# When the modulation vectors of a four-layer encoder are computed, on which engine, and into which PSUM banks an output projection is summed

## The chip, the core and the metric

One core of one Trainium2 chip runs the whole step; nothing is shared with other cores. The metric is the device time of one execution in microseconds (us), the median of several runs. The engines named below are TensorE (PE, with PEld for its weight loads), VectorE (DVE), ScalarE (ACT), GpSimd (POOL) and SyncE (SP, which issues the transfers).

## The reference, cut to what matters

The kernel computes one inference step of a four-layer encoder for two sequences at once: a prompt of 256 tokens and a sample of 64, so 320 token columns of width 1024. Each layer is three sub-layers: a gated feed-forward net (ffn1), a token mixer (retention in layers 0 and 3, pooling in layer 1, attention in layer 2) and a second feed-forward net (ffn2). Every sub-layer is modulated by three vectors that come from the conditioning vector of its sequence:

```
c_act = silu(c)
mod = c_act @ ada_w[i] + ada_b[i]                       # 9 vectors of 1024 a layer
sh1, sc1, g1, shm, scm, gm, sh2, sc2, g2 = split(mod, 9)
h = rmsnorm(x, norm_g[i, 0]) * (1.0 + sc1) + sh1
x = x + 0.5 * g1 * swiglu(h, ffn1_w_in[i], ffn1_w_out[i])
h = rmsnorm(x, norm_g[i, 1]) * (1.0 + scm) + shm        # then the mixer, gm; then sc2, sh2, g2
```

All is float32. With 36 vectors of 1024 x 1024 weights, the modulation reads 288 weight tiles of 512 KB, beside 690 of the main weights.

## The kernel before, in words

**The stream.** All main weights are laid out as 690 chunks, each of eight 128 x 128 tiles, in the order in which TensorE uses them; a chunk is one transfer of 512 KB (`Stream.load`, L265). Six raw buffers hold what has landed. A float32 product is made of three faster products of a high and a low part: ScalarE rounds a raw chunk to its high part `hi` (L277), VectorE subtracts to get the low part `lo` (L284), and TensorE does three matmuls per tile (`mm3`, L379 to L381). The splits run three chunks ahead of the use. `next_tiles` is the kernel's metronome: at the first tile of a chunk it splits `hi` three chunks ahead and runs what is due (`tick`), and in the middle of the chunk it does the same for `lo`.

**Sub-layers.** There are twelve, numbered 0 to 11 here. Each has an input stretch (projections from the normalised `x`, held as `xh` and `xl`, 320 token columns and two shift columns) and an output stretch (eight output blocks m = 0 to 7, each summed over all k tiles, then added to `x` in `residual`, L558 on VectorE). In a feed-forward net the input stretch has 44 chunks and the output stretch 22. In an input stretch VectorE reads each finished pair of PSUM banks (L593), multiplies (L614) and takes low parts (L415). The retention and the attention use `out_projection`: its first four blocks are summed in two cuts of k, so that the late k tiles can still be in the making, and the blocks 4 to 7 follow one at a time.

**PSUM.** The eight banks are two pairs `mm` (four banks, handed out pair by pair), three banks `wk`, and one bank `ada`. Tiles are tracked by pair: an instruction that writes one bank of a pair waits for the readers of the pair. `four_banks` puts blocks 0 and 1 in one pair and 2 and 3 in the other. `bank` takes a whole pair and uses its first half.

**Modulation.** A vector v = 3n (shift), 3n + 1 (gain) or 3n + 2 (gate) of sub-layer n is made in one of two ways, one weight tile at a time, eight tiles a vector. On TensorE (`ada_pe`, L460): four matmuls of 32 columns each into the `ada` bank, and at the end a transpose on VectorE (L465). On VectorE (`ada_dve`, L475): two multiply-and-sum instructions over 1024 columns, one for each sequence. The first two vectors are made on TensorE before the stream starts. `ada_plan` decides the rest: each vector has a due chunk, each chunk has some room for VectorE tiles (`ROOM_IN` in an input stretch, `ROOM_OUT` in an output stretch, `ROOM_RET` in a retention's input stretch), and a vector goes to VectorE if the room up to its due chunk holds its eight tiles; otherwise it goes to TensorE, spread evenly over the time left. The plan before puts four vectors, 4, 16, 19 and 28, on TensorE, and the other 30 on VectorE.

**Shift columns.** `shift_columns` (ACT L521, DVE L522) writes the next sub-layer's shift vector into two columns of `xh` and `xl`. It is called at the first tile of the output stretch.

Of the kernel before, what the change touches and what calls it, by code (L numbers as in the profile page):

```python
# [11 lines left out]
F32 = mybir.dt.float32  # L12
# [7 lines left out]
P = 128  # L20
D = 1024
KT = D // P
# [26 lines left out]


PE_STEP = 1
ROOM_IN = {"ffn": 0.42, "poo": 0.0, "att": 0.0}
ROOM_OUT = {"ffn": 0.6, "ret": 0.5, "poo": 0.0, "att": 0.3}
ROOM_RET = (1, 0, 0, 0, 0, 0, 0, 0, 0, 1, 2, 0)

# [13 lines left out]
def sub_tiles(kind, layer):  # L69

    j = layer // 3
    out = []
    if kind in ("ffn1", "ffn2"):
        wi, wo = kind + "_w_in", kind + "_w_out"
        for m in range(FT):
            for kt in range(KT):
                out.append((wi, layer, kt, m * P))
                out.append((wi, layer, kt, DFF + m * P))
        for m in range(KT):
            for kt in range(FT):  # L80
                out.append((wo, layer, kt, m * P))
    elif kind == "ret":
        for h in range(RH):
            for base, n, w in ((0, 2, RDK), (D, 2, RDK), (2 * D, 4, RDV), (4 * D, 4, RDV)):
                for m in range(n):
                    for kt in range(KT):
                        out.append(("ret_w_in", j, kt, base + h * w + m * P))
        out += [("ret_w_out", j, kt, m * P) for m, kt in out_order(4 * RH, RET_EARLY)]
    elif kind == "pool":
        for g in range(4):  # L90
            for kt in range(2):
                for m in range(2):
                    out.append(("pool_w", (j, g), kt, m * P))
    else:
        for hp, part in att_columns():
            for base in ((0, D), (2 * D,))[part]:
                for kt in range(KT):
                    out.append(("att_w_qkv", j, kt, base + hp * P))
        out += [("att_w_o", j, kt, m * P) for m, kt in out_order(NPAIR, ATT_EARLY)]
    return out  # L100


def out_order(nk, early):

    cuts = (0, *early, nk)
    out = [(m, kt) for a, b in zip(cuts, cuts[1:]) for m in range(4) for kt in range(a, b)]
    return out + [(m, kt) for m in range(4, KT) for kt in range(nk)]


def att_columns():  # L110

    out = [(0, 0), (1, 0), (0, 1), (1, 1)]
    for hp in range(2, NPAIR):
        out += [(hp, 0)] if hp >= ATT_LATE else [(hp, 0), (hp, 1)]
    return out + [(hp, 1) for hp in range(ATT_LATE, NPAIR)]


def chunk_starts(subs):
    starts, n = [], 0
    for kind, layer in subs:  # L120
        starts.append(n)
        n += len(sub_tiles(kind, layer)) // 8
    return starts, n


def ada_plan(subs):


    starts, total = chunk_starts(subs)
    due, room = {}, [0.0] * total  # L130
    for n, (kind, layer) in enumerate(subs):
        w_in = {"ffn1": 44, "ffn2": 44, "ret": 48, "att": 24, "pool": 0}[kind]
        due[3 * n + 2] = starts[n] + w_in
        if n + 1 < len(subs):
            due[3 * n + 3] = starts[n] + w_in
            due[3 * n + 4] = starts[n] + w_in
        size = len(sub_tiles(kind, layer)) // 8
        for c in range(size):
            if 3 <= c < size - 2:
                own = ROOM_IN if c < w_in else ROOM_OUT  # L140
                room[starts[n] + c] = ROOM_RET[c % 12] if kind == "ret" and c < w_in else own[kind[:3]]
    order = sorted(due)
    got = np.concatenate([[0.0], np.cumsum(room)])
    plan = {}
    on_pe, done = [], 0
    for v in order:
        if got[due[v] - 2] >= done + KT:
            for t in range(KT):
                done += 1
                c = max(1, int(np.searchsorted(got, done - 1e-6)) - 1)  # L150
                plan.setdefault(c, []).append(("d", v, t))
        else:
            on_pe.append(v)
    at = 1.0
    for i, v in enumerate(on_pe):
        rest = min((due[u] - 2 - at) / (KT / PE_STEP * (k + 1)) for k, u in enumerate(on_pe[i:]))
        for kt in range(0, KT, PE_STEP):
            plan.setdefault(int(at), []).append(("a", v, kt))
            at += max(0.0, rest)
    return plan  # L160


def ada_layout(subs):

    return {v: what for todo in ada_plan(subs).values() for what, v, _ in todo} | {0: "a", 1: "a"}
# [147 lines left out]
class Kernel:  # L313
# [74 lines left out]
        return self.banks()[:, 0]  # L388

    def four_banks(self):  # L390
        t = (self.banks(), self.banks())
        return [t[i // 2][:, i % 2] for i in range(4)]

    def twins(self, name, dt=F32, n=2):
        return self.twin.tile([P, n, TW], dt, tag="twin", name=name)
# [57 lines left out]
    def ada_pe(self, v, kts):  # L453
        nc = self.nc
        for kt in kts:
            if kt == 0:
                self.ada_ps = self.adap.tile([P, 256], F32, tag="ada", name="ada")
            t = self.stream.take(("a", v, kt))
            for j in range(4):
                nc.tensor.matmul(out=self.ada_ps[32 * j:32 * j + 32, :], lhsT=self.cpad[:, kt, :],  # L460
                                 rhs=t[:, 256 * j:256 * j + 256], start=kt == 0, stop=kt == KT - 1)
            self.stream.load()
        if kts[-1] == KT - 1:
            tr = self.small.tile([P, KT, 32], F32, tag="adat", name="adat", bufs=1)
            nc.vector.transpose(out=tr.rearrange("p t s -> p (t s)"), in_=self.ada_ps)  # L465
            o = self.mod.tile([P, KT, 2], F32, tag=f"mod{v % 3}", name="mod")
            self.ada_end(v, o, tr[:, :, 0:2])
# [135 lines left out]
    def ffn(self, n):  # L603
        nc = self.nc
        hid = []

        def evac(ps):
            g, u = self.normed(ps)
            self.shifted(g, AF.Silu)
            self.shifted(u)  # L610
            self.at(2, lambda: combine(g[:, 0:NT], u[:, 0:NT]))

        def combine(g, u):
            nc.vector.tensor_tensor(out=u, in0=u, in1=g, op=ALU.mult)  # L614
            self.parts_later(u, hid.append)

        self.begin()
        for m in range(FT):
            ps = self.banks()
            for kt in range(KT):  # L620
                for i in range(2):
                    hi, lo = self.stream.next_tile()
                    self.mm3(ps[:, i, 0:NB], hi, lo, self.xh[:, kt, 0:NB], self.xl[:, kt, 0:NB], kt == 0, kt == KT - 1)
            self.after_norm(1, lambda ps=ps: evac(ps))
        for m in range(KT):
            po = self.bank()
            for kt in range(FT):
                hi, lo = self.stream.next_tile()
                if m == 0 and kt == 0:
                    if n + 1 < len(self.subs):  # L630
                        self.shift_columns(n + 1)
                if kt >= len(hid):
                    self.flush()
                h, l = hid[kt]
                self.mm3(po[:, 0:NT], hi, lo, h, l, kt == 0, kt == FT - 1)
            self.residual(n, m, po)
# [174 lines left out]
    def out_projection(self, n, nk, early, operands):  # L811

        ps = dict(enumerate(self.four_banks()))
        for i, (m, kt) in enumerate(out_order(nk, early)):
            hi, lo = self.stream.next_tile()
            if i == 0 and n + 1 < len(self.subs):
                self.shift_columns(n + 1)
            if operands[kt] is None:
                self.flush()
            if kt == 0 and m >= 4:  # L820
                ps[m] = self.bank()
            h, l = operands[kt]
            self.mm3(ps[m][:, 0:NT], hi, lo, h, l, kt == 0, kt == nk - 1)
            if kt == nk - 1:
                self.residual(n, m, ps[m])
# [386 lines left out]
```

## Time and profile before

| what | us |
|---|---|
| median of 3 runs | 2734.98 (2732.3 to 2736.49) |
| the profiled execution's own time | 2739.32 |
| its span, first to last instruction | 2737.5 |
| PE busy | 2693.6 (98%) |
| DVE busy | 2132.6 (78%) |
| ACT busy | 1332.4 (49%) |

The times in the rows below come from the one profiled execution. Its span leaves 1.8 us of its own time outside, and its own time is 4.3 us above the median of the runs. Matmuls overlap: one lasts 0.31 us, and the next starts 0.15 us after it, so the distance between starts says what a matmul costs. In a timeline the release in brackets names the idle time before an instruction and what ended it.

### The profile page before, as it was taken

The numbers are of one execution on the slowest core, as the hardware profiler recorded it, in microseconds if no ns is written. First come the engines' busy times: TensorE is split into PE (matmuls) and PEld (weight loads), VectorE is DVE, ScalarE is ACT, GpSimd is POOL, SyncE is SP. The second block draws the span as 40 slices with busy tenths as digits, with TensorE's granted clock in tenths as the row PEclk, the third lists the DMA queues.
The fourth block names the chain that finished last, engine by engine and source line by source line (L and its number), as shares of the span: only waits on it lengthen the run. The fifth ranks groups of instructions, "written<-read, shape, count | busy, mean of one in ns | idle before, by whom it ended". The sixth has DMA issues, their size and how long they took to land.

```text
span 2737.5 us, 46828 instructions
## 1 busy us (share of the span) xinstructions
PE 2693.6 (98%) x18328; PEld 2595.7 (95%) x18328; DVE 2132.6 (78%) x3606; ACT 1332.4 (49%) x2393; POOL 69.9 (3%) x141
## 2 busy tenths in 40 slices
PE   7999999999999999999999999999999999999999
PEld 5999988899999998999999988999999998889999
DVE  5879777788888887889788777788888877756553
ACT  4554454445535544554554455555455444544552
POOL 0000000000000002000000021000000000000000
PEclk9999999999999999999999999999999999999999
DMA  8667555666676674666666644466766655544442
GB/s 330 228 226 244 167 187 171 207 206 218 217 230 209 215 232 161 226 218 234 207 215 224 208 156 129 155 218 209 237 197 213 226 185 170 174 150 146 150 153 94
DMA packets 150109, 543.64 MB, mean 199 GB/s; under 512 B 17872, under 2 KB 19152, under 8 KB 149632
## 3 DMA queue, kind: packets, MB, share of 16 engines
q1 hardware_dynamic: 142272, 517.51, 57.4%
q0 software_dynamic: 6464, 21.82, 2.4%
q8 instruction: 144, 2.36, 0.4%
q10 hardware_dynamic: 1152, 1.31, 0.1%
q14 instruction: 77, 0.63, 0.1%
HBM read 528.13 MB, written 12.44 MB: 197 GB/s over the span
## 4 chain that ended last, share of the span: by engine, by line
PE 58%; DVE 2%; ACT 1%; issue 1%; DVEq 0%; ACTq 0%
PE mm L379 18%; PE mm L380 18%; PE mm L381 18%; PE wk L723 1%; PE wk L754 1%; DVE lo L284 0%; DVE pr L1000 0%; ACT pr L994 0%; PE wk L1053 0%; PE wk L957 0%; PE wk L707 0%; DVE xt L558 0%; DVE xl L505 0%; PE ada L460 0%; PE wk L1035 0%
## 5 line engine op out<-in xcount | busy, mean ns | idle before, releaser
L379 PE MATMUL mm<-xh,hi 128*128 128x322 f32 x3776 | 1198.6, 317 | 3.1 <-DVE xt L558 1.2
L380 PE MATMUL mm<-xl,hi 128*128 128x322 f32 x3776 | 1171.7, 310 | 0.1
L381 PE MATMUL mm<-xh,lo 128*128 128x322 f32 x3776 | 1169.8, 310 | 0.0
L277 ACT ACTIVATE hi<-raw 128x1024 fp32r<-128x1024 f32 x690 | 726.8, 1057 | 732.6 <-PE mm L380 635.0
L284 DVE TENSOR_TENSOR lo<-raw,hi 128x1024 fp32r<-128x1024 f32 x690 | 840.9, 1222 | 249.9 <-ACT hi L277 238.9
L379 PEld LDWEIGHTS mm<-xh,hi 128*128 128x128 f32 x3776 | 713.0, 189 | 27.2 <-issue 21.9
L380 PEld LDWEIGHTS mm<-xl,hi 128*128 128x128 f32 x3776 | 714.4, 189 | 5.1 <-issue 4.8
L381 PEld LDWEIGHTS mm<-xh,lo 128*128 128x128 f32 x3776 | 714.5, 189 | 0.0
L475 DVE SCALAR_TENSOR_TENSOR junk<-raw,cb 128x1024 f32<-128x1024 f32 x480 | 586.4, 1222 | 8.6
L379 PE MATMUL mm<-part,hi 128*128 128x320 f32 x1728 | 537.6, 311 | 7.9 <-DVE xt L558 7.9
L381 PE MATMUL mm<-part,lo 128*128 128x320 f32 x1728 | 536.2, 310 | 0.0
L380 PE MATMUL mm<-part,hi 128*128 128x320 f32 x1728 | 533.7, 309 | 0.1
L599 ACT ACTIVATE twin<-twin 128x256 f32<-128x256 f32 (+1 forms) x944 | 328.8, 418 | 193.9 <-DVE twin L593 193.9
L379 PEld LDWEIGHTS mm<-part,hi 128*128 128x128 f32 x1728 | 325.8, 189 | 15.7 <-DVE xt L558 9.4
L380 PEld LDWEIGHTS mm<-part,hi 128*128 128x128 f32 x1728 | 326.0, 189 | 1.3 <-issue 1.0
L381 PEld LDWEIGHTS mm<-part,lo 128*128 128x128 f32 x1728 | 326.3, 189 | 0.0
L593 DVE TENSOR_TENSOR twin<-mm,rx 128x644 f32<-128x644 f32 (+1 forms) x240 | 195.4, 814 | 75.3 <-PE mm L381 74.6
L499 ACT ACTIVATE xh<-xt,mod 128x256 fp32r<-128x256 f32 x192 | 71.1, 421 | 204.5 <-DVE xt L558 202.9
L558 DVE SCALAR_TENSOR_TENSOR xt<-mm,mod,xt 128x256 f32<-128x256 f32 (+1 forms) x176 | 59.3, 378 | 61.5 <-PE mm L381 61.5
L412 ACT ACTIVATE part<-twin 128x320 fp32r<-128x320 f32 x176 | 81.2, 461 | 48.3 <-DVE twin L614 48.3
L614 DVE TENSOR_TENSOR twin<-twin 128x320 f32<-128x320 f32 x176 | 85.7, 490 | 23.2 <-ACT twin L599 18.8
L415 DVE TENSOR_TENSOR part<-twin,part 128x320 fp32r<-128x320 f32 x176 | 85.4, 485 | 1.1 <-ACT part L412 1.1
(162 smaller groups left out, 1130.2 us busy)
## 6 DMA issues: line engine op xcount, KB each, us to landing
raw<-in_wmain SPq DMA_DIRECT2D x690, 512.0 KB, 3.8
raw<-in_wada SPq DMA_DIRECT2D x288, 512.0 KB, 4.2
out_ret_p<-st POOLq DMA_DIRECT2D x16, 256.0 KB, 2.5
out_ret_s<-st POOLq DMA_DIRECT2D x16, 256.0 KB, 3.8
s<-in_s POOLq DMA_DIRECT2D x6, 512.0 KB, 6.3
fb<-in_fb POOLq DMA_DIRECT2D x8, 384.0 KB, 4.0
xt<-in_xt SPq DMA_DIRECT2D x1, 1280.0 KB, 10.3
out_v_o<-twin POOLq DMA_DIRECT2D x8, 160.0 KB, 4.0
```

Of the source, the lines that this page charges most:

```text
L277: self.nc.scalar.activation(out=hi, in_=t, func=AF.Copy)
L284: self.nc.vector.tensor_tensor(out=lo, in0=t, in1=hi.bitcast(F32), op=ALU.subtract)
L379: t.matmul(out=out, lhsT=hi, rhs=xh, start=start, stop=False)
L380: t.matmul(out=out, lhsT=hi, rhs=xl, start=False, stop=False)
L381: t.matmul(out=out, lhsT=lo, rhs=xh, start=False, stop=stop)
L412: self.nc.scalar.activation(out=hi, in_=src, func=AF.Copy)
L415: self.nc.vector.tensor_tensor(out=lo, in0=src, in1=hi.bitcast(F32), op=ALU.subtract)
L475: nc.vector.scalar_tensor_tensor(out=self.junk, in0=t, scalar=1.0, in1=self.cb[:, s], op0=ALU.mult, op1=ALU.mult, accum_out=self.modv[v][: ...
L499: self.nc.scalar.activation(out=self.xh[:, t, b:e], in_=self.x[:, t, b:e], func=AF.Copy, scale=g[:, t, s:s + 1])
L593: self.nc.vector.tensor_tensor(out=t[:, :, 0:NB], in0=ps[:, :, 0:NB], in1=self.rx[:, None, 0:NB].to_broadcast([P, n, NB]), op=ALU.mult)
L599: self.nc.scalar.activation(out=t[:, b:e], in_=t[:, b:e], func=func, bias=t[:, NT + s:NT + s + 1])
L614: nc.vector.tensor_tensor(out=u, in0=u, in1=g, op=ALU.mult)
```

## The change

It has three parts. The first concerns the plan: the room for VectorE tiles in a feed-forward input stretch goes from 0.42 to 0.54 per chunk; a shift vector is due three chunks before its sub-layer's predecessor ends instead of at the start of the output stretch (where that is later); and vectors are taken in the order of their due chunks rather than of their numbers. The plan that results puts all vectors but the first two on VectorE: 34 vectors, 272 tiles (before 240). A feed-forward input stretch then holds 22 VectorE tiles (before 17 or 18) and an output stretch 12 as before; the attention's output stretch holds 2 (before 1), in chunks 420 and 424 (before 422). The second: `shift_columns` is called at the first tile of block 7, the last output block, instead of at the first tile of the output stretch. The third: `four_banks` puts blocks 0 and 2 in one pair and 1 and 3 in the other, and block 4 of `out_projection` is summed in the `ada` bank (`spare_bank`), which is idle then.

```
-ROOM_IN = {"ffn": 0.42, "poo": 0.0, "att": 0.0}
+ROOM_IN = {"ffn": 0.54, "poo": 0.0, "att": 0.0}
...
+        size = len(sub_tiles(kind, layer)) // 8
         due[3 * n + 2] = starts[n] + w_in
         if n + 1 < len(subs):
-            due[3 * n + 3] = starts[n] + w_in
+            due[3 * n + 3] = starts[n] + max(w_in, size - 3)
             due[3 * n + 4] = starts[n] + w_in
...
-    order = sorted(due)
+    order = sorted(due, key=lambda v: (due[v], v))
...
     def four_banks(self):
+
         t = (self.banks(), self.banks())
-        return [t[i // 2][:, i % 2] for i in range(4)]
+        return [t[i % 2][:, i // 2] for i in range(4)]
+
+    def spare_bank(self):
+        return self.adap.tile([P, 512], F32, tag="ada", name="spare")
...
-                self.ada_ps = self.adap.tile([P, 256], F32, tag="ada", name="ada")
+                self.ada_ps = self.adap.tile([P, 512], F32, tag="ada", name="ada")[:, 0:256]
...
-                if m == 0 and kt == 0:
+                if m == KT - 1 and kt == 0:
                     if n + 1 < len(self.subs):
                         self.shift_columns(n + 1)
...
-            if i == 0 and n + 1 < len(self.subs):
+            if m == KT - 1 and kt == 0 and n + 1 < len(self.subs):
                 self.shift_columns(n + 1)
...
             if kt == 0 and m >= 4:
-                ps[m] = self.bank()
+                ps[m] = self.spare_bank() if m == 4 else self.bank()
```

Four lines were added above most of the code, so L593 of the kernel before is L597 of the changed one, L475 is L479, and so on; `mm3` keeps its lines.

On TensorE, at the end of the first chunk of sub-layer 0 (`mm_307` is a pair of banks, `hi_265` and `hi_289` the first two chunks, `ada_340` the bank of vector 4), there stood before:

```order
L379 MATMUL mm_307<-xh_111,hi_265 128x322
L380 MATMUL mm_307<-xl_112,hi_265 128x322
L381 MATMUL mm_307<-xh_111,lo_267 128x322
L460 MATMUL ada_340<-raw_275,cpad_115 32x256 [waits DMAHW2_49,PE_49]
L460 MATMUL ada_340<-raw_275,cpad_115 32x256 x3
L379 MATMUL mm_307<-xh_111,hi_289 128x322 [waits Activation_49]
L380 MATMUL mm_307<-xl_112,hi_289 128x322
```

and now:

```order
L379 MATMUL mm_307<-xh_111,hi_265 128x322
L380 MATMUL mm_307<-xl_112,hi_265 128x322
L381 MATMUL mm_307<-xh_111,lo_267 128x322
L379 MATMUL mm_307<-xh_111,hi_289 128x322 [waits Activation_49]
L380 MATMUL mm_307<-xl_112,hi_289 128x322
```

The four matmuls of a modulation tile are gone, here and at 31 other chunk starts; nothing takes their place on this engine.

On TensorE in the attention's output projection, where block 0 ends and block 1 goes on, and where block 2 ends and block 3 goes on (before, `mm_17734` is the pair of blocks 0 and 1, `mm_17735` that of 2 and 3):

```order
L381 MATMUL mm_17734<-part_17939,lo_17686 128x320
L379 MATMUL mm_17734<-part_17553,hi_17662 128x320 [waits DVE_49]
L380 MATMUL mm_17734<-part_17553,hi_17662 128x320
...
L381 MATMUL mm_17735<-part_17939,lo_17762 128x320
L379 MATMUL mm_17735<-part_17553,hi_17736 128x320 [waits DVE_49]
L380 MATMUL mm_17735<-part_17553,hi_17736 128x320
```

and now, from the end of block 0 (`mm_17640` is the pair of blocks 0 and 2, `mm_17641` that of 1 and 3):

```order
L381 MATMUL mm_17640<-part_17848,lo_17592 128x320
L379 MATMUL mm_17641<-part_17459,hi_17568 128x320
...
L381 MATMUL mm_17641<-part_17848,lo_17592 128x320
L379 MATMUL mm_17640<-part_17459,hi_17642 128x320 [waits DVE_49]
...
L381 MATMUL mm_17640<-part_17848,lo_17666 128x320
L379 MATMUL mm_17641<-part_17459,hi_17642 128x320 [waits DVE_49]
```

Blocks 1 and 3 went on only behind the readers of the block that had just ended. Now block 1 goes on at once, block 2 waits for the readers of block 0, and block 3 for those of block 1: one block later in each case.

On VectorE at the end of the attention (`pr_17333` before and `pr_17239` now are the scores of the last pair of heads, `part` the parts of a finished pair, `lo` a chunk's low part), before:

```order
L997 TENSOR_SCALAR pr_17333<-pr_17333,sm_17782 128x256
L405 TENSOR_TENSOR part_17809<-wk_17796,part_17809 128x320 [waits DMASW3_49,Activation_49]
L284 TENSOR_TENSOR lo_17848<-raw_17360,hi_17824 128x1024 [waits DMAHW7_49,PE_49,Activation_49]
L1000 SCALAR_TENSOR_TENSOR pr_17333<-wk_17857,rq_17596,fs_17326 64x384 [waits DMASW2_49,DMASW3_49,PE_49,Pool_49]
L1000 SCALAR_TENSOR_TENSOR pr_17333<-wk_17857,rq_17596,fs_17326 64x384
```

and now:

```order
L1001 TENSOR_SCALAR pr_17239<-pr_17239,sm_17686 128x256
L409 TENSOR_TENSOR part_17713<-wk_17700,part_17713 128x320 [waits DMASW3_49,Activation_49]
L479 SCALAR_TENSOR_TENSOR junk_110,mod_17716<-raw_17266,cb_301 128x1024 [waits DMAHW1_49]
L479 SCALAR_TENSOR_TENSOR junk_110,mod_17716<-raw_17266,cb_301 128x1024 [waits DVE_49]
L284 TENSOR_TENSOR lo_17757<-raw_17347,hi_17733 128x1024 [waits DMAHW2_49,PE_49,Activation_49]
L1004 SCALAR_TENSOR_TENSOR pr_17239<-wk_17766,rq_17502,fs_17232 64x384 [waits DMASW2_49,DMASW3_49,PE_49,Pool_49]
L1004 SCALAR_TENSOR_TENSOR pr_17239<-wk_17766,rq_17502,fs_17232 64x384
```

A modulation tile, two instructions, now stands between the finished part and the scores of the sample for the last pair of heads. Before, the only such tile of this output stretch stood behind the residual of block 0.

## Rows read from the trace of the kernel before

**Rows 1.** The page, part 1: busy us, share of the span, instructions of each engine.

```profile
PE 2693.6 (98%) x18328; PEld 2595.7 (95%) x18328; DVE 2132.6 (78%) x3606; ACT 1332.4 (49%) x2393; POOL 69.9 (3%) x141
```

**Rows 2.** The page, part 4: shares of the chain that ended last, by engine.

```profile
PE 58%; DVE 2%; ACT 1%; issue 1%; DVEq 0%; ACTq 0%
```

**Rows 3.** Timeline of PE around one modulation tile: start us, us, what, idle before.

```profile
908.54 0.30 PE L381 MATMUL mm<-xh,lo 128*128 128x322 f32 x1
908.78 0.64 PE L460 MATMUL ada<-raw,cpad 128*32 128x256 f32 x8
909.35 0.41 PE L379 MATMUL mm<-xh,hi 128*128 128x322 f32 x1
909.60 0.31 PE L380 MATMUL mm<-xl,hi 128*128 128x322 f32 x1
```

**Rows 4.** Windows of PE: stretch, its length, busy us (matmuls), granted clock, DMA.

```profile
62.73:73.49 10.76, 10.76 (x74) 1.00 0.73 249
854.89:905.10 50.21, 50.21 (x338) 1.00 0.65 211
912.99:962.45 49.46, 49.46 (x338) 1.00 0.63 211
1820.74:1899.65 78.91, 78.91 (x531) 1.00 0.66 213
```

**Rows 5.** Waits of PE in the output projections of sub-layers 1, 10 and 7.

```profile
PE mm L379 <- DVE xt L558: 2.6, 2, 1.8
PE mm L379 <- DVE xt L558: 1.5, 2, 0.8
PE mm L379 <- DVE xt L558: 3.8, 2, 3.0
```

**Rows 6.** Timeline of PE and DVE in the output projection of sub-layer 1.

```profile
536.47 0.31 PE L381 MATMUL mm<-part,lo 128*128 128x320 f32 x1
537.83 0.67 DVE L558 SCALAR_TENSOR_TENSOR xt<-mm,mod,xt 128x256 f32<-128x256 f32 x2
538.56 0.41 PE L379 MATMUL mm<-part,hi 128*128 128x320 f32 x1 [1.78 <-DVE xt L558]
```

**Rows 7.** Windows of PE in the half-clock stretches behind two waits.

```profile
539.40:542.80 3.40, 3.40 (x15) 0.50 0.77 277
1720.40:1727.20 6.80, 5.70 (x21) 0.50 0.41 141
```

**Rows 8.** Windows of DVE: input and output stretch of sub-layer 9, input stretch of 11.

```profile
1992.40:2133.80 141.40, 120.71 (x170) 1.00 0.65 207
2133.80:2211.00 77.20, 68.69 (x114) 1.00 0.72 235
2515.10:2656.50 141.40, 84.36 (x102) 1.00 0.44 148
```

**Rows 9.** Lines of DVE in the input stretch of sub-layer 9: busy us, mean ns.

```profile
L284 DVE TENSOR_TENSOR lo<-raw,hi 128x1024 fp32r<-128x1024 f32 x40 | 48.9, 1222 | 11.1 <-ACT hi L277 9.8
L475 DVE SCALAR_TENSOR_TENSOR junk<-raw,cb 128x1024 f32<-128x1024 f32 x33 | 40.3, 1222 | 0.6
L593 DVE TENSOR_TENSOR twin<-mm,rx 128x644 f32<-128x644 f32 x20 | 16.5, 827 | 6.4 <-PE mm L381 6.3
L614 DVE TENSOR_TENSOR twin<-twin 128x320 f32<-128x320 f32 x21 | 10.2, 489 | 2.6 <-ACT twin L599 2.3
L415 DVE TENSOR_TENSOR part<-twin,part 128x320 fp32r<-128x320 f32 x21 | 10.2, 485 | 0.2 <-ACT part L412 0.2
```

**Rows 10.** Timeline of DVE around one modulation tile.

```profile
58.12 1.22 DVE L475 SCALAR_TENSOR_TENSOR junk<-raw,cb 128x1024 f32<-128x1024 f32 x1
60.54 0.82 DVE L593 TENSOR_TENSOR twin<-mm,rx 128x644 f32<-128x644 f32 x1
```

**Rows 11.** Timeline of DVE and PE at the end of the attention.

```profile
1708.31 0.42 DVE L997 TENSOR_SCALAR pr<-pr,sm 128x384 f32<-128x384 f32 x1
1709.97 0.87 PE L1035 MATMUL wk<-cst,pr 128*128 128x128 f32 x6
```

More of the change, by code (lines that the diff above doesn't have):

```diff
@@ L132, in ada_plan @@
         w_in = {"ffn1": 44, "ffn2": 44, "ret": 48, "att": 24, "pool": 0}[kind]
+        size = len(sub_tiles(kind, layer)) // 8
         due[3 * n + 2] = starts[n] + w_in
         if n + 1 < len(subs):
-            due[3 * n + 3] = starts[n] + w_in
+            due[3 * n + 3] = starts[n] + max(w_in, size - 3)
             due[3 * n + 4] = starts[n] + w_in
-        size = len(sub_tiles(kind, layer)) // 8
         for c in range(size):
```

## The prediction, written before the changed kernel ran

> **What bounds the kernel now.** I read the busy shares first: TensorE 98%, VectorE 78%, ScalarE 49% [rows 1]. Then the chain that ended last: TensorE holds 58% of it and no other engine over 2% [rows 2]. So time goes where TensorE's own work goes, plus the few places where it waits. Three things on TensorE are not the main product. (a) Modulation tiles, which I looked for in its timeline [rows 3]. (b) A slower beat of the main matmuls in some stretches, seen by comparing windows that hold equal numbers of matmuls [rows 4]. (c) Waits in the three out projections with two cuts, from the list of waits [rows 5], and behind two of them a granted clock of one half [rows 7]. After that I looked at the engine that gets more work, VectorE: how full its stretches are [rows 8], and of what [rows 9].
>
> **The change part by part.**
>
> *Modulation tiles leave TensorE.* A matmul of the main product starts 0.15 us after the one before. Across a modulation tile the distance is 908.54 to 909.35, 0.81 us, and the next one is 0.25 (909.35 to 909.60) [rows 3]: 0.66 + 0.10 = 0.76 us lost per tile. The plan takes away four vectors of eight tiles: 32 x 0.76 = 24.3 us. All stand inside the stream, where TensorE is busy throughout, so the whole of it counts. Their transfers stay: the same 512 KB tiles go through the same raw buffers and are only read by VectorE.
>
> *The slower beat.* In sub-layer 3, 338 matmuls last 50.21 us behind the first modulation tile of the stretch and 49.46 us behind the second: 1.5% [rows 4]. The same alternation goes through every feed-forward input stretch that holds modulation tiles: slow after an odd one, normal after an even one. There are ten such slow stretches, the first at 62.73 us and the last, of 78.91 us, ending at 1899.65 [rows 4]; they make up 344 us. Without modulation tiles I expect none: 344 x 0.015 = 5.1 us. I know no cause, only the coincidence, so the lower bound is 0.
>
> *The pairing of the blocks.* TensorE waits 2.6, 1.5 and 3.8 us in the three output projections, six waits, all for the residual of the block that has just ended [rows 5]. The case at 538.56 shows how: block 2's last matmul starts at 536.47, its residual only at 537.83, and block 3 stands until 538.56, though it writes another bank of the pair [rows 6]. From start to start that is 2.09 instead of 0.15 us, 1.94 lost where 1.78 is listed; and the matmul behind a wait costs about 0.10 more, as in rows 3. So the six cost 7.9 + 6 x 0.26 = 9.5 us. Behind the wait of 1.78 us the clock is granted at 0.50 (1.2 of 2.4 GHz) for 3.4 us, in which 15 matmuls run; behind the one of 3.0 us for 6.8 us, with 21 matmuls in 5.70 busy us [rows 7]. At the full beat these would take 2.2 and 3.1 us: 1.2 + 2.6 = 3.8 us more. The waits of 0.77 left the clock alone. Now a block waits for the residual of the block before the last, one block (3 us in the retention, 1.8 in the attention) later. The residual at 537.83 was 1.2 us late, so I take all six waits as gone, and the clock's falls with them: 9.5 + 3.8 = 13.3 us. Bounds: half of it, 6.6, if block 3 still finds block 1's residual late, and 13.3.
>
> *The spare bank.* Block 4 never waits in the trace of before: no matmul at its start is among the six. Taken alone it is worth 0; with the new pairing it keeps block 4 from waiting for block 2's residual. Bounds 0 and 1.1 us, a wait of 0.77 as in rows 5 with its 0.3 of restart.
>
> *VectorE gets 32 tiles more, where?* A tile costs 2.42 us of its queue (58.12 to 60.54) [rows 10]. In an input stretch it is busy 84.36 of 141.40 us without tiles, and 120.71 with 33 multiply instructions, 16.5 tiles [rows 8, 9]: 2.2 us each. With 22 tiles it will be 84.4 + 48.4 = 132.8 of 141.4, 94%. The output stretches keep their 12 tiles at 68.69 of 77.20, 89% [rows 8], and show no wait of TensorE for them. `lo` is made three chunks (10.5 us) ahead and a bank pair has 7 us until its next use, so a backlog of one tile hides. I charge 0. If the cover were gone, each wait costs as above, 1.1 to 5.8 us.
>
> The Trainium skill would charge more here: VectorE: DVE Perf Modes, section "The DRAIN you can't avoid", says that the next operation does not start until the pipeline has emptied, so that whole durations add up. By that the rows of the input stretch, 48.9 + 16.5 + 10.2 + 10.2 = 85.8 us [rows 9], and 22 tiles of 2 x 1.222 give 139.6 of 141.4 us, before any wait. The trace differs: those four rows and the 40.3 of the multiplies sum to 126.1 us, while the engine was busy in 120.71 [rows 8], so neighbours overlap.
>
> *One of the added tiles meets a chain.* In the attention's output stretch the tile of chunk 420 now stands ahead of the last pair's sample scores: 2.4 us on a chain that ended on VectorE at 1708.73, while TensorE came for it (the second of the two turns that start at 1709.97) at about 1710.4 [rows 11]. Slack 1.7, so 0.7 us is lost; less the gap of 0.4 that VectorE had in front of the scores, 0.3 to 0.4. I take 0.4; bounds 0 and 2.4. The tile that leaves chunk 422 stood ahead of block 1's residual, for which block 3 now waits.
>
> *Shift columns.* The same two small instructions, later; they are needed 22, 16 or 8 tiles on. The shortest lead, 8 tiles of three matmuls of 0.15 us, is 3.5 us, and in front can stand one `lo` (1.222) and one tile (2.42): 3.6 us. So 0, with 0.1 us as the other end. Pooling takes the new pairing too: its first output bank waits for one more ScalarE copy, 0 to 1.1 us; I take 0.
>
> *Sum.* 24.3 + 5.1 + 13.3 - 0.4 = 42.3 us. On the profiled execution's own 2739.3 us that makes 2697.0. The runs have a median of 2735.0, 4.3 below it, so for the runs I forecast 2735.0 - 42.3 = 2692.7, say **2693 us**.
>
> **The rivals.**
>
> *Part of the bank waits or the slow beat stays.* For it: VectorE was late by a whole residual at 537.83 [rows 6], and I do not know what makes the beat. Against it: with one block of distance that lateness is covered, and a stretch with no modulation tile on TensorE keeps the beat. Half the waits back is -6.6, the beat kept -5.1: 2698 to 2705 us.
>
> *VectorE becomes the bound of the input stretches.* By whole durations (the rule above) it would be at 139.6 of 141.4, and what it waits for others no longer fits: 6.4 + 2.6 us of idle time in front of two of its rows [rows 9] would push each of seven input stretches over by up to 7 us. For it: 94% leaves little. Against it: the overlap, and output stretches that run at 89% without a wait. Between 10 and 45 us back: 2703 to 2738 us.
>
> *Slower: the evacuations come late and the clock falls.* One mechanism: a pair of banks in an input stretch is read too late, TensorE stands as at 538.56 and then runs at half clock as in rows 7. One such event costs 2.0 + 1.2 = 3.2 us. It decides when VectorE's backlog passes the 7 us between uses of a pair, three tiles in a row. To turn the gain of 42 round takes 14 events, two in each of the seven input stretches; three in each are 21 x 3.2 = 67 us, 2760 us. Against it: the plan places at most two tiles in neighbouring chunks there, and before shows no wait of TensorE in an input stretch of a feed-forward net.
>
> **How the numbers follow.** The forecast (2684 to 2698) has 0.70; the first rival 0.19; VectorE as the bound 0.08; slower 0.03. The range goes to the far ends of the first rival, 2705, and some way into the second, 2712, and below to 2684, where the waits cost more than I counted or VectorE's later work runs earlier: 2684 to 2712. A measurement of this kernel can tell 0.2%, 5.5 us, from no change. Faster by more: the forecast, the first rival and most of the second, 0.95. Same, out of the second: 0.02. Slower: 0.03.
>
> **What would show it.** Right: no L464 matmul after the first 35 us; windows of 338 matmuls of 49.5 us everywhere in input stretches; no wait of `mm` for `xt` in the output projections; clock 1.00 at the ends of sub-layers 1 and 7; VectorE busy about 133 of 141 us in an input stretch. Wrong: waits of TensorE for L597 (the evacuation) or `lo` inside input stretches, or a wait at block 3.

## The result, and the profile after

The changed kernel takes 2700.97 us (median; 2700.73 to 2702.38), the kernel before, beside it on the same chip, 2735.73 us (2732.3 to 2739.15). The ratio is 0.9875, 95% interval 0.9863 to 0.9887: faster. The profiled execution of the changed kernel took 2702.38 us with a span of 2700.6; the span of before was 2737.5, so 36.9 us have gone between the two traces. The forecast was 2693 us; the time lies in the range, 8 us above the forecast.

The page's busy times after (part 1, as [rows 1]):

```profile
PE 2661.8 (99%) x18072; PEld 2584.2 (96%) x18072; DVE 2193.4 (81%) x3730; ACT 1326.4 (49%) x2393; POOL 69.6 (3%) x141
```

TensorE has 256 records fewer, 32 tiles of four matmuls with two records each, and is busy 31.8 us less. VectorE has 60.8 us more, which is less than 32 tiles of 2.42 us make (77.4): its instructions overlap.

The beat is even now. Two windows of PE in the input stretch of sub-layer 3 (columns as in [rows 4]):

```profile
839.80:889.20 49.40, 49.40 (x338) 1.00 0.74 233
889.20:938.60 49.40, 49.40 (x337) 1.00 0.71 226
```

Before, the first part of this stretch took 50.21 us for the same number [rows 4]. The out projection of sub-layer 1, in the timeline of DVE and PE (as [rows 6]):

```profile
526.11 0.67 DVE L562 SCALAR_TENSOR_TENSOR xt<-mm,mod,xt 128x256 f32<-128x256 f32 x2
...
527.73 0.31 PE L379 MATMUL spare<-part,hi 128*128 128x320 f32 x1
```

Block 2's residual comes at 526.11, while block 3 runs on, and block 4 starts in the spare bank without a wait. In the list of PE's waits from 475 to 560 us one row is left, and in sub-layer 10 none:

```profile
PE mm L379 <- ACT xh L525: 0.3, 1, 0.3
```

That one is new: sub-layer 2 waits for its shift columns. VectorE in the input and the output stretch of sub-layer 9 (windows, columns as in [rows 8]), and its lines in the input stretch:

```profile
1957.50:2098.90 141.40, 131.85 (x194) 1.00 0.70 227
2098.90:2176.10 77.20, 67.50 (x110) 1.00 0.73 238
```

```profile
L479 DVE SCALAR_TENSOR_TENSOR junk<-raw,cb 128x1024 f32<-128x1024 f32 x44 | 53.8, 1222 | 0.8
L284 DVE TENSOR_TENSOR lo<-raw,hi 128x1024 fp32r<-128x1024 f32 x40 | 48.8, 1219 | 4.5 <-ACT hi L277 4.1
L597 DVE TENSOR_TENSOR twin<-mm,rx 128x644 f32<-128x644 f32 x20 | 16.5, 824 | 1.1 <-PE mm L381 1.1
L618 DVE TENSOR_TENSOR twin<-twin 128x320 f32<-128x320 f32 x21 | 10.2, 488 | 2.6 <-ACT twin L603 2.6
L419 DVE TENSOR_TENSOR part<-twin,part 128x320 fp32r<-128x320 f32 x21 | 10.2, 485 | 0.2 <-ACT part L416 0.2
```

VectorE is busy in 131.85 of 141.40 us with 22 tiles, and TensorE waits for it nowhere in these stretches. What is left in front of its rows is smaller than before [rows 9]: 4.5 us at `lo` where 11.1 were, 1.1 at L597 where 6.4 were. The five rows alone sum to 139.5 us; they fit into 131.85 only because neighbours overlap.

New waits stand at the end of the attention. Here are the first three of the five rows in the list of PE's waits from 1670 to 1725 us (us in total, times, longest); the first two of them stand in the place of the third group of [rows 5]:

```profile
PE mm L379 <- DVE xt L562: 2.1, 1, 2.1
PE mm L379 <- ACT xh L525: 1.9, 1, 1.9
PE wk L1039 <- ACT vt L973: 1.3, 1, 1.3
```

Rows chosen from the timeline of DVE, ACT and PE there (start us, us, what; in brackets the idle time before it):

```profile
1695.92 0.08 DVE L479 DVE_READ_ACCUMULATOR junk<-raw,cb 128x1 f32 x1
1695.92 0.67 DVE L562 SCALAR_TENSOR_TENSOR xt<-spare,mod,xt 128x256 f32<-128x256 f32 x2
1696.43 0.75 ACT L503 ACTIVATE xh<-xt,mod 128x256 fp32r<-128x256 f32 x2 [4.10 <-DVE xt L562]
1697.44 1.04 ACT L277 ACTIVATE hi<-raw 128x1024 fp32r<-128x1024 f32 x1
1698.52 1.23 DVE L284 TENSOR_TENSOR lo<-raw,hi 128x1024 fp32r<-128x1024 f32 x1 [0.46 <-ACT hi L277]
1699.67 0.67 DVE L562 SCALAR_TENSOR_TENSOR xt<-mm,mod,xt 128x256 f32<-128x256 f32 x2
1700.48 0.39 PE L379 MATMUL mm<-part,hi 128*128 128x320 f32 x1 [2.07 <-DVE xt L562]
...
1703.41 0.67 DVE L562 SCALAR_TENSOR_TENSOR xt<-mm,mod,xt 128x256 f32<-128x256 f32 x2
1703.92 0.75 ACT L503 ACTIVATE xh<-xt,mod 128x256 fp32r<-128x256 f32 x2 [1.69 <-DVE xt L562]
1704.93 1.04 ACT L277 ACTIVATE hi<-raw 128x1024 fp32r<-128x1024 f32 x1
1705.88 0.20 ACT L525 ACTIVATE xh<-mod 128x16 fp32r<-128x16 f32 x1
1706.13 0.41 PE L379 MATMUL mm<-xh,hi 128*128 128x322 f32 x1 [1.90 <-ACT xh L525]
```

Here the reader sees a loop over two engines. A residual on VectorE (1695.92) lets ScalarE make the next operand and, behind it in its queue, the split `hi` (1697.44); `hi` lets VectorE make `lo` (1698.52), and only behind `lo` comes the next residual (1699.67). One turn is 3.75 us, while TensorE needs 3.51 us for a block. A modulation tile ends at 1695.92, ahead of block 4's residual; nothing behind it can catch up. Block 7 waits 2.07 us for the bank of block 5. The shift columns (L525), which used to be made at the first tile of the projection, now stand behind the last `hi`, and sub-layer 8's first matmul waits 1.90 us for them. Behind that the clock is granted at one half, 1.2 of 2.4 GHz (window of PE, columns as in [rows 7]):

```profile
1707.10:1710.50 3.40, 3.40 (x15) 0.50 0.49 154
```

Where the 36.9 us came from, from start to start of the chunks' first matmuls in both traces:

| place | gained, us | forecast |
|---|---|---|
| modulation tiles and even beat, all sub-layers | 29.6 | 29.4 |
| output projections of sub-layers 1 and 10 | 6.7 | 6.3 |
| attention, waits of blocks 1 and 3 with clock | 6.9 | 6.9 |
| attention, before its output projection | 1.6 | 0 |
| attention, tile of chunk 420 | -1.4 | -0.4 |
| attention, block 7's wait | -2.2 | 0 |
| sub-layer 8's start: wait, then half clock | -2.2, -1.7 | 0 |
| sub-layer 2's start | -0.6 | 0 |

They add up to 36.7. The -1.4 is from the experiment without that tile, below. The fourth row is a stretch in which the traces of the other kernels lie 0.4 to 2.7 us below before; its cause stays open.

### The profile page after: what moved, and what is told of

The parts are those of the page before. It is cut to its first block, busy times and chain, and to the rows that moved or that the text cites. A ratio compares the mean times of both kernels' runs of the same rounds, so it can differ in the third digit from the quotient of the medians.

```text
span 2700.6 us, 46421 instructions
## 1 busy us (share of the span) xinstructions
PE 2661.8 (99%) x18072; PEld 2584.2 (96%) x18072; DVE 2193.4 (81%) x3730; ACT 1326.4 (49%) x2393; POOL 69.6 (3%) x141
## 5 line engine op out<-in xcount | busy, mean ns | idle before, releaser
L479 DVE SCALAR_TENSOR_TENSOR junk<-raw,cb 128x1024 f32<-128x1024 f32 x544 | 664.3, 1221 | 9.5
L379 PE MATMUL mm<-part,hi 128*128 128x320 f32 x1688 | 521.9, 309 | 2.1 <-DVE xt L562 2.1
L381 PE MATMUL mm<-part,lo 128*128 128x320 f32 x1688 | 522.8, 310 | 0.0
L380 PE MATMUL mm<-part,hi 128*128 128x320 f32 x1688 | 519.4, 308 | 0.1
L379 PEld LDWEIGHTS mm<-part,hi 128*128 128x128 f32 x1688 | 316.6, 188 | 5.2 <-issue 4.5
L380 PEld LDWEIGHTS mm<-part,hi 128*128 128x128 f32 x1688 | 316.9, 188 | 1.3 <-issue 1.0
L381 PEld LDWEIGHTS mm<-part,lo 128*128 128x128 f32 x1688 | 317.0, 188 | 0.0
L597 DVE TENSOR_TENSOR twin<-mm,rx 128x644 f32<-128x644 f32 (+1 forms) x240 | 194.8, 812 | 35.6 <-PE mm L381 35.2
L618 DVE TENSOR_TENSOR twin<-twin 128x320 f32<-128x320 f32 x176 | 85.8, 489 | 24.3 <-ACT twin L603 22.0
```

What stands on the lines that cost most here:

```text
L379: t.matmul(out=out, lhsT=hi, rhs=xh, start=start, stop=False)
L380: t.matmul(out=out, lhsT=hi, rhs=xl, start=False, stop=False)
L381: t.matmul(out=out, lhsT=lo, rhs=xh, start=False, stop=stop)
L479: nc.vector.scalar_tensor_tensor(out=self.junk, in0=t, scalar=1.0, in1=self.cb[:, s], op0=ALU.mult, op1=ALU.mult, accum_out=self.modv[v][: ...
L597: self.nc.vector.tensor_tensor(out=t[:, :, 0:NB], in0=ps[:, :, 0:NB], in1=self.rx[:, None, 0:NB].to_broadcast([P, n, NB]), op=ALU.mult)
```

## The experiments

Each ran beside the kernel before, whose median was 2736.19 us (2733.76 to 2738.29) beside the first four and 2733.41 (2732.26 to 2736.22) beside the next three.

**The pairing of blocks undone.** The changed kernel with

```
-        return [t[i % 2][:, i // 2] for i in range(4)]
+        return [t[i // 2][:, i % 2] for i in range(4)]
...
-                ps[m] = self.spare_bank() if m == 4 else self.bank()
+                ps[m] = self.bank()
```

> The changed kernel with the old pairing of blocks (0 with 1, 2 with 3) and no spare bank. Theory (the loop residual - operand parts on ScalarE - low part paces the end of the attention, so the pairing gains nothing lasting there): the retentions lose what the pairing gave, 4.65 us in sub-layer 1 and 2.06 in sub-layer 10; the attention's output stretch gets its two waits of before back but loses most of the new ones at block 7 and at the shift columns, 0 to 2 us on balance: 2708 to 2710 us for the run, 6.7 to 8.7 above the changed kernel. Rival (each wait stands for itself, and the new ones come from the tile in chunk 424 alone): attention worse by 5.8 us more, 2713 to 2714 us.

Measured: 2709.4 us (2708.72 to 2709.9), ratio 0.9904 (0.9889 to 0.9919): 8.4 above the changed kernel, though the pairing had brought 6.7 + 6.9 us to their places. PE's waits from 1675 to 1730 us:

```profile
PE mm L379 <- ACT xh L525: 1.9, 1, 1.9
PE mm L379 <- DVE xt L562: 1.9, 2, 1.1
```

Sub-layers 1 and 10 lose 4.2 and 2.1 us again, the attention only 1.5 (0.9 of it before its output projection): with the old pairing the waits of blocks 1 and 3 come back, block 7's goes, and the one for the shift columns stays. So in the attention of the changed kernel, which has a modulation tile at chunk 424 and late shift columns, what the pairing gains at one block is given back a few blocks later. That this need not be so shows below, where the tiles are gone.

**The pairing alone.** The kernel before with the first of the two lines above in its new form (no spare bank, no other change).

> The kernel before with the new pairing of blocks alone (plan, shift columns and banks otherwise as before; block 4 takes a pair of its own). Theory of the paced loop: sub-layers 1 and 10 lose 4.65 and 2.06 us, the attention 1 to 3 us: 8 to 10 us below before, about 2726. Rival (the pairing is worth its full 13.3 us): 2722. In both the modulation tiles on TensorE and the slow beat stay.

Measured: 2730.01 us (2725.49 to 2730.85), ratio 0.9976 (0.9967 to 0.9986), so 6.2 us, where 8 to 10 were expected. Sub-layer 10 gains its 2.05, the attention 5.2 (2.1 of it before its output projection, 3.1 in it). Of the two waits in the attention one is left, in the list of PE's waits from 1650 to 1760 us:

```profile
PE mm L379 <- DVE xt L558: 2.0, 1, 2.0
```

It stands in front of block 3, which waits for block 1's residual, and that stands behind the modulation tile of chunk 422; the clock falls behind it too. This costs 3.8 us against the kernels without a tile in that place, and so the pairing brings its full 6.9 us in the attention only together with the new plan, which moves this tile. Sub-layer 1 gains only 1.06: what blocks 1 and 3 gain is taken back by a modulation tile on TensorE. The timeline there (SPq and POOL: the issue of a transfer):

```profile
538.87 0.33 SPq L265 DMA_DIRECT2D raw<-in_wada  x1
539.04 0.54 POOL L841 DMA_DIRECT2D win<-in_win  x1 [3.79 <-PE mm L381]
...
547.83 0.64 PE L460 MATMUL ada<-raw,cpad 128*32 128x256 f32 x8 [1.98 <-DMA raw<-in_wada]
```

This tile's transfer was issued beside the 896 KB that pooling loads, and came 8.9 us later, where the median is 4.2. In the kernel before it came as late (issued 539.66, landed 548.16), but TensorE arrived at 550.40, held up by the very waits that the pairing removes. That the two transfers slow each other is not tested. The wait costs the half clock again (granted 0.51 in the 3.40 us from 548.90). In the changed kernel no modulation tile is left on TensorE there, and the gain stays: the parts need each other.

**No tiles in the attention's output, and its shift columns early.** The changed kernel with

```
-ROOM_OUT = {"ffn": 0.6, "ret": 0.5, "poo": 0.0, "att": 0.3}
+ROOM_OUT = {"ffn": 0.6, "ret": 0.5, "poo": 0.0, "att": 0.0}
...
-            if m == KT - 1 and kt == 0 and n + 1 < len(self.subs):
+            if (i == 0 if nk == NPAIR else m == KT - 1 and kt == 0) and n + 1 < len(self.subs):
```

> The changed kernel with two edits in the attention's output stretch: no modulation tile there (room 0), and the shift columns written at its first tile again. Theory (the tile of chunk 424 delays the residual of block 4 and so of block 5, for which block 7 waits; the shift columns stand in ScalarE's queue behind a late residual; the clock falls behind these two waits): the 2.2, 2.1 and 1.7 us of chunks 426 to 428 go, 6.0 us, 2695 us for the run. Rival (the loop is late by itself, with no tile in it): block 7 still waits, 2697 to 2699 us.

Measured: 2694.12 us (2692.84 to 2697.32), ratio 0.985 (0.9836 to 0.9865); it beats both kernels. Its timeline of VectorE, residuals of the attention's blocks 3 to 7:

```profile
1686.22 0.67 DVE L562 SCALAR_TENSOR_TENSOR xt<-mm,mod,xt 128x256 f32<-128x256 f32 x2
1689.97 0.67 DVE L562 SCALAR_TENSOR_TENSOR xt<-spare,mod,xt 128x256 f32<-128x256 f32 x2
1693.72 0.67 DVE L562 SCALAR_TENSOR_TENSOR xt<-mm,mod,xt 128x256 f32<-128x256 f32 x2
1697.47 0.67 DVE L562 SCALAR_TENSOR_TENSOR xt<-mm,mod,xt 128x256 f32<-128x256 f32 x2
1701.22 0.67 DVE L562 SCALAR_TENSOR_TENSOR xt<-mm,mod,xt 128x256 f32<-128x256 f32 x2
```

The loop's 3.75 us are still there. Without a tile in it the residuals fall only 0.24 us further behind with each block, and no block waits for one; sub-layer 7 takes 181.06 us instead of 187.79 (1.15 of the difference lies before its output projection), sub-layer 8 234.17 instead of 235.85, and the clock does not fall between them.

**Only the shift columns early.** The second of these edits alone.

> The changed kernel with the shift columns of the sub-layer after the attention written at the first tile of its output stretch again; the modulation tiles stay. Theory: the 1.9 us in front of the first matmul of sub-layer 8 goes, the 2.1 us at block 7 stay; whether the clock still falls behind block 7's wait is open: 2697.4 us if it does not, 2699 if it does. Rival (another late thing takes the place of the shift columns, such as the high part of block 0 of the next operand): no change, 2701.

Measured: 2698.89 us (2698.05 to 2702.96), ratio 0.9871 (0.9855 to 0.9887). In its list of PE's waits from 1660 to 1720 us

```profile
PE mm L379 <- DVE xt L562: 2.1, 1, 2.1
```

stays, and the one for `xh` is gone with the half clock, as in the first of the two cases forecast: sub-layer 8 takes 234.17 us, and the output stretch of sub-layer 7 44.26 instead of 46.03.

**Only the tiles gone.** The first of these edits alone.

> The changed kernel without modulation tiles on VectorE in the attention's output stretch (they move to the stretches behind); the shift columns stay at the last output block. Theory (two mechanisms, added up): the tile of chunk 420 cost 1.4 us ahead of the last sample scores and the tile of chunk 424 made block 7 wait 2.1 us for block 5; both go, while the first matmul of sub-layer 8 still waits about 1.9 us for the shift columns, which ScalarE makes late, with the half clock behind it: sub-layer 7 at about 183.5 us, sub-layer 8 at 235.8, 2697 us. Rival (the tiles alone made ScalarE late, so that the late shift columns do no harm by themselves): the wait for the shift columns and the half clock go too: sub-layer 7 at 181 to 182 us, sub-layer 8 at 234.2, 2694 us.

Measured: 2698.4 us (2696.28 to 2699.46), ratio 0.9868 (0.9851 to 0.9884). The list of PE's waits from 1660 to 1725 us is the mirror image,

```profile
PE mm L379 <- ACT xh L525: 1.8, 1, 1.8
```

and block 7 waits for nothing; sub-layer 7 takes 183.99 us, sub-layer 8 235.83. So these are two mechanisms, and they add up: of the 46.03 us of the output stretch the early columns take away 1.77, the missing tiles 3.79, and both edits together 5.58. The loop's own lateness, without a tile, is enough to make late shift columns cost 1.8 us and the clock behind them.

**No spare bank.** The changed kernel with `ps[m] = self.bank()` for block 4 too.

> The changed kernel with block 4 of the output projections in the next bank of the two pairs again, so without the spare bank; everything else as changed. Theory (the spare bank is worth nothing alone, and no tail of the attention hangs on it): block 4 waits for block 2, which lies one block back, and with the pairs in rotation block 7 still waits for block 5, so the wait of 2.1 us at the attention's last block, the 1.9 us for the shift columns and the half clock behind them stay: 2701 us, with sub-layers 1, 7 and 10 within 0.5 us of 286.95, 187.8 and 286.6. Rival (the bank is what keeps block 4 from standing): a wait of 0.8 to 1.1 us with its restart at block 4 in the three sub-layers, 2703 to 2704 us. Second rival (by shifting the order of the banks the spare one caused the wait at block 7): sub-layer 7 gets 2 us shorter, 2697 us.

Measured: 2702.61 us (2701.08 to 2704.31), ratio 0.9884 (0.9869 to 0.9898): not told apart from the changed kernel. Sub-layers 1 and 10 are the same to 0.01 us. In the attention the wait for a residual moves from block 7, where the theory had it, to block 6 and is 1.6 instead of 2.1 us, with small waits around it; the output stretch takes 46.03 us in both kernels, and the 1.2 us by which the sub-layer is longer lie before it. Neither rival held.

**What makes the slow beat.** The changed kernel with useless matmuls at the local chunks 8 and 24 of input stretches, in a function of their own:

```
+            mm(out=t[q:q + 32, 0:256], lhsT=self.cpad[:, 0, :], rhs=self.cb[:, 0, 0:256], start=True, stop=True)
```

> The changed kernel with useless matmuls put into feed-forward sub-layers at their local chunks 8 and 24, each group into a bank that nothing reads, to find what makes the slower beat (50.21 us against 49.46 us for 338 matmuls). Sub-layer 2: four matmuls on 32 columns each of the array, as a modulation tile had them (128x32, 256 columns, float32); 3: two of them; 5: one; 6: three; 9: eight; 8: one matmul of 128x128 by 256 columns, float32; 11: three matmuls as in the main product (bfloat16). Theory (a group on parts of the array turns some state over, each time): chunks 8 to 23 of sub-layer 2 at 3.59 us each instead of 3.53, and chunks 24 to 43 back at 3.53; with 8 (two groups) and with the full-width matmuls no change. What counts, matmuls or groups, is read from sub-layers 3, 5, 6: if each single matmul turns it over, only odd numbers (one, three) do and four don't. Rival (the slower beat came from the modulation tiles' transfers or waits, not from their matmuls): every chunk but the one with the insertion stays at 3.53 us. The time as a whole: 2701 us and some 0.8 us for each of 12 small insertions, and up to 1 us for each stretch with the slower beat: 2708 to 2716 us.

Measured: 2715.05 us, one execution. Windows of PE of 42.40 us behind chunk 8 of sub-layers 2, 3, 5 and 6 (four, two, one and three narrow matmuls) and of 9 and 8 (eight narrow ones; a full-width one); the second row is sub-layer 2 behind chunk 24:

```profile
592.00:634.40 42.40, 42.40 (x285) 1.00 0.68 220
652.00:694.40 42.40, 42.40 (x290) 1.00 0.73 233
829.00:871.40 42.40, 42.40 (x286) 1.00 0.68 221
1092.00:1134.40 42.40, 42.40 (x286) 1.00 0.69 224
1328.00:1370.40 42.40, 42.40 (x286) 1.00 0.72 231
1990.00:2032.40 42.40, 42.40 (x290) 1.00 0.73 233
1752.00:1794.40 42.40, 42.40 (x290) 1.00 0.70 227
```

285 or 286 matmuls instead of 290 in the same time, at a granted clock of 1.00: one to four narrow matmuls slow the main ones behind them by 1.5%, and a second such group ends it. No transfer and no wait came with these, so the rival falls. A single narrow one does as much as four; eight, a full-width one and the three of the main type (sub-layer 11, float32r in the kernel) leave 290.

This holds for the input stretches, with 322 columns. In the kernel before, windows of PE in the output stretch of sub-layer 0 (320 columns), ahead of and behind its modulation tile at 249.15, show no slower beat:

```profile
225.00:246.00 21.00, 21.00 (x146) 1.00 0.73 237
254.00:275.00 21.00, 21.00 (x146) 1.00 0.77 250
```

In that kernel the slow beat of sub-layer 8 also ends with its input stretch, with no second group, and a tile in the first chunk of sub-layers 0 and 8 leaves none. The prediction's "slow after an odd one, normal after an even one" therefore does not hold as it stands for these two.

**Which groups turn it.** Other groups at the same places.

> The changed kernel with other groups of useless matmuls at the same two places of feed-forward sub-layers (local chunks 8 and 24). A narrow one has 128x32 weights and 256 columns of float32. Sub-layer 2: five narrow ones on column groups 0, 1, 2, 3, 0; 3: twelve, three times 0 to 3; 5: two, both on group 0; 6: four in falling order 3, 2, 1, 0; 8: one on group 0 with 64 columns only; 9: three, all on group 0; 11: one with 64 weight columns. Theory (each round of at most four narrow matmuls on column groups not yet used turns the beat over once, as one to four of them did and eight, two rounds, did not): slow chunks (3.59 us) behind chunk 8 in sub-layers 3 (three rounds), 8 and 9 (three rounds) and, if the order counts for nothing, 6; 3.53 us in 2 and 5 (two rounds); sub-layer 11 is open, slow if a half-width group counts as a round. Rival (what counts is how long the group keeps the engine off the main product, up to 0.66 us slow, over 1 us not): 5, 6, 8 and perhaps 9 slow, 2 and 3 not. The time as a whole: 2708 to 2722 us.

Measured: 2717.7 us, one execution. Windows of PE of 42.40 us behind chunk 8 of sub-layers 2 (five), 3 (twelve), 5 (two on one column group), 6 (four, falling), 8 (one, short), 9 (three on one group), 11 (one of half width):

```profile
592.00:634.40 42.40, 42.40 (x290) 1.00 0.69 219
829.00:871.40 42.40, 42.40 (x290) 1.00 0.67 219
1092.00:1134.40 42.40, 42.40 (x290) 1.00 0.70 222
1329.00:1371.40 42.40, 42.40 (x285) 1.00 0.74 228
1753.50:1795.90 42.40, 42.40 (x285) 1.00 0.69 226
1990.00:2032.40 42.40, 42.40 (x290) 1.00 0.72 230
2513.50:2555.90 42.40, 42.40 (x286) 1.00 0.44 147
```

The theory misses twice: twelve and three on one group, three rounds each, leave the beat even, so rounds are not counted odd and even. The rival misses 5 and has 9 only as a perhaps. What holds for all cases is that one round of narrow matmuls, each column group used once, turns the beat, and a group of several rounds that meets an even beat does not. Among narrow groups a rule by time fits as well: from chunk start to chunk start, those that turned it cost 0.4 to 0.8 us, those that did not 1.2 to 1.6 us. What state is turned is open.

## Why the prediction was nearly right, and where it failed

*Modulation tiles and beat.* The two terms held together: 29.6 us against 24.3 + 5.1. The beat had only a coincidence behind it, with 0 as its lower end, so that its size came out was partly luck; the dummies show that the narrow matmuls themselves made it.

*Pairing.* All six waits and both falls of the clock are gone, for 6.7 + 6.9 us against 13.3. The lateness of a residual was read rightly from [rows 6] as one that a block of distance covers, save in the attention: there the pairing alone leaves block 3's wait, and 3.8 of the 6.9 us come from the plan, which moves the tile of chunk 422. What was not looked at: in the attention the residuals were already a 3.75 us loop against blocks of 3.51. In the timeline of DVE before, block 3's residual still waits for TensorE, and from there the loop runs:

```profile
1729.66 0.68 DVE L558 SCALAR_TENSOR_TENSOR xt<-mm,mod,xt 128x256 f32<-128x256 f32 x2 [0.72 <-PE mm L381]
1733.41 0.67 DVE L558 SCALAR_TENSOR_TENSOR xt<-mm,mod,xt 128x256 f32<-128x256 f32 x2
```

The removed waits had been giving the loop time: without them block 3's residual comes late even where there is no tile (1686.22 above, no idle time in front of it).

*VectorE.* Charged at 0, and TensorE has no new wait for it in an input stretch: 131.85 us busy where 132.8 were worked out, so the rival with VectorE as the bound fell. (One wait of 0.60 us for the evacuation stands in sub-layer 5's input stretch in both traces; that before shows none there was misread.) The Trainium skill, VectorE: DVE Perf Modes, section "The DRAIN you can't avoid", has the next operation start only once the pipeline is empty. The same paragraph adds that an operation which is not held starts earlier. The prediction took the first half alone; by that the lines of the input stretch, 139.5 us and 3.6 more for the accumulator reads, would not have fitted into 141.4. The trace agrees with the second half: the residual at 1699.67 starts 1.15 us after a `lo` that lasts 1.23.

*"So 0, with 0.1 us as the other end"* (shift columns) is the step that failed most. The lead of 8 tiles was compared with what could stand in front of the two instructions on VectorE; but the first of them is ScalarE's, queued behind operands that wait for a late residual, then behind `hi`. It cost a wait of 1.9 us (2.2 with the restart), 1.7 us of half clock behind it, and 0.6 at sub-layer 2.

*"I take 0.4; bounds 0 and 2.4"* (the tile of chunk 420) measured 1.4 us: inside its bounds, mis-sized. The same tile rate put a second one into chunk 424, which the sum does not mention; it cost 2.2 us at block 7.

*Spare bank.* Taken at 0; without it the median lies 1.6 us higher, half of the 3.2 us by which that kernel's runs differ, and the output stretches take the same time.

The first rival (part of the waits stays, 2698 to 2705 us) is where the time fell, though not by its mechanism: the old waits went, and two new ones came. The terms missed add up to 7.7 us (1.0 + 2.2 + 3.9 + 0.6); against them stand 0.6 us by which the large terms came out higher and the 1.6 us in front of the attention's output projection. That leaves 5.5 us; by the two traces the sum of 42.3 was 5.4 too high. By the medians it was 7.5 too high: the profiled execution of before lies 3.6 us above the median beside it, that of after 1.4 above its own. With the two causes taken away the kernel runs in 2694.12 us, about the forecast.

## What to carry to other kernels

When a wait is removed, look at the loop that the waiting engine was pacing: compare the period of the helpers' chain (here 3.75 us over VectorE and ScalarE) with the bottleneck's own (3.51), and if the chain is slower, price everything behind it as late, above all small instructions moved to its end. Place filler work by each stretch's slack, not by one rate for a kind of stretch: about five tiles more in each long input stretch brought no new wait, and two in a short tail cost 3.6 us. An instruction moved later has to be followed through every engine that it crosses, in queue order.

## What the runs showed of the hardware

A single narrow float32 matmul (128x32 weights) between the main ones of an input stretch (322 columns) leaves those behind it 1.5% slower at full granted clock, 286 instead of 290 in 42.40 us, until the next such group or the end of the stretch; what state this is stays open. VectorE's neighbours overlap: 143.1 us of listed durations in 131.85 busy us.
